# Moving the rebuild of x to VectorE and three small copies to GpSimd in a recurrent layer

## The chip, the cores and the metric

The kernel runs on one NeuronCore of one Trainium2 chip. The metric is device time in microseconds (us), from runs of the whole program on that core. A core has a matrix engine (TensorE, in the profile PE, with its weight loads as PEld) and four engines that matter beside it here: VectorE (DVE), ScalarE (ACT), GpSimd (POOL) and SyncE (SP), which only issues transfers in this kernel. Each engine works through its own list of instructions strictly in the order in which the list was built, and the lists wait for one another by semaphores. An instruction at the head of a list that has to wait holds up everything behind it on that engine.

## The reference, cut to what matters

One inference step of a two-layer decoder: 1024 prompt tokens and 8 sample tokens, so 1032 columns in all, at a width of 1024. Layer 0 is a recurrent block, layer 1 attention; each is followed by an MLP. The change sits in layer 0:

```python
u = x @ w_in
gate, xr = jnp.split(u, 2, axis=-1)
xc, conv_new = causal_conv(xr, conv_prev, conv_w, conv_b)     # width 4, and the last 3 rows as new state
r = sigmoid(xc @ w_a + b_a);  i = sigmoid(xc @ w_x + b_x)     # in 4 blocks of 256 channels
a = exp(-8 * r * softplus(-lam))
u = sqrt(1 - a*a) * (i * xc)
h = scan(h_t = a_t * h_{t-1} + u_t)                           # and the last h as new state
out = (h * gelu(gate)) @ w_out
```

Products are computed in full single precision by splitting each operand into a rounded high part and the rest (low part) and adding three products: high with high, high with low, low with high.

## The kernel before

Everything is kept transposed: 128 channels on the partitions, 1032 tokens along the row. The width is eight such tiles, called m = 0 to 7. A product of one output tile is 8 (or, in a gate block, 2) pieces along the depth times 3 passes times 3 chunks of 344 tokens, and its three chunks lie in three PSUM banks. There are two sets of three banks, "bP" and "bS, bS, bT", and the products take them in turn: while TensorE fills one set, the other has to be emptied, or TensorE waits.

The recurrent layer is a list of stages, written out by hand in `LRU` (lines 55 and 56), run in the order of that list:

- `x` m (`xr_stage`): the product of the input with w_in for tile m, 72 matmuls. VectorE empties the banks (line 1127) and GpSimd starts the convolution from the result (line 1128, three chunks).
- `c` m (`conv`): the other taps of the convolution on VectorE (line 1133 for the prompt, 1137 for the sample tokens), two small copies of state rows (lines 1134 and 1135), and the split of xc into high and low, the high part on ScalarE (line 253), the low on VectorE (line 254).
- `g` k (`gates`): four products of 18 matmuls each, for the two gates of the tiles 2k and 2k+1. ScalarE empties the banks with the sigmoid (line 1161).
- `r` k (`recur`): for two tiles: x = high + low (line 1170), i * x (1171), tanh, exp and squares on ScalarE (1173, 1175, 1180), a product on VectorE (1181), the square root (1183), the scan (1186 to 1189), and the copy of the last state (1190). The tanh writes over the tile that holds x, so it waits until line 1171 has read it.
- `o` m (`gate_out`): the gate product, 72 matmuls, emptied by VectorE (line 1199), then gelu and the product with the scan.

The stages in the order in which they are written are: c1 c0 x4 g0 c2 c3 r0 c4 x5 g1 c5 r1 x7 x6 g2 r2 c7 o5 c6 o0 o1 o3 g3 r3 o6 o2 o4 o7. A scheduler then builds the list of each engine from this program: it may put an instruction of a later stage ahead of one of an earlier stage, by its own estimate of when operands are ready, and by the priority that some stages ask for. So a change in one line can move others on all lists.

Weights arrive as tiles `raw` of 512 KB through two buffers in turn (`fetch`, line 159, issued on SP's queue). ScalarE rounds each into `wh` (line 165), an engine subtracts into `wl` (line 166: VectorE, for one unit in this stretch GpSimd), and then the buffer is free for the next transfer. The state rows leave through the same SP queue: `o_conv` twice (lines 1211 and 1212, they need the copies of all eight `c` stages; the last tile to come is m = 6) and `o_h` (line 1213). In the program these three stand behind r3; where they stand in SP's list is up to the scheduler.

Of the kernel before, what the change touches and what calls it, by code (L numbers as in the profile page):

```python
# [13 lines left out]
ALU = mybir.AluOpType  # L14
# [5 lines left out]
SEQ = 1024  # L20
NS = 8
T = SEQ + NS
# [37 lines left out]
def trunk(ctx: ExitStack, tc: tile.TileContext, I, O):  # L60
    nc = tc.nc
    pe, act, dve, pool, sp = nc.tensor, nc.scalar, nc.vector, nc.gpsimd, nc.sync
# [30 lines left out]
    def A(s="a"):  # L93
        return ap.tile([P, T], F32, tag="A", name=nm(s))
# [4 lines left out]
    def S(s="s"):  # L99
        return small["pool"].tile([P, CH], F32, tag="S", name=nm(s))  # L100
# [24 lines left out]
    def cs(c):  # L125
        return slice(c * CH, (c + 1) * CH)
# [12 lines left out]
    def V(n, m=0):  # L139
        o, _ = VEC[n]  # L140
        return vec[:, o + m:o + m + 1]
# [34 lines left out]
    for o in [("x", m) for m in range(4)] + LRU:  # L176
        if o[0] == "g":
            units.append(("gate", o[1], I["w_gate"][o[1]], W))
        elif o[0] in "xo":
            m = o[1] + (8 if o[0] == "x" else 0)  # L180
# [71 lines left out]
    def split_act_dve(hi, lo, src, sl, eng=dve):  # L252
        act.copy(r_(hi[:, sl]), src)
        eng.tensor_tensor(r_(lo[:, sl]), src, hi[:, sl], ALU.subtract)
# [834 lines left out]
    cst = cp.tile([P, M8, 4, NS], F32, name="cst")  # L1089
# [3 lines left out]
    cvp = cp.tile([P, M8, 3], F32, name="cvp")  # L1093
    hno = cp.tile([P, M8, 1 + NS], F32, name="hno")
# [23 lines left out]
    ys = {}  # L1118
# [11 lines left out]
    def conv(m):  # L1130
        xr, xc = xrc.pop(m)
        for d, w in ((1, "cw2"), (2, "cw1"), (3, "cw0")):
            dve.scalar_tensor_tensor(xc[:, d:SEQ], xr[:, 0:SEQ - d], V(w, m), xc[:, d:SEQ], ALU.mult, ALU.add)
        dve.tensor_copy(cst[:, m, 3, :], xr[:, SEQ:T])
        dve.tensor_copy(cvp[:, m, :], xr[:, SEQ - 3:SEQ])
        for k, w in ((2, "cw2"), (1, "cw1"), (0, "cw0")):
            dve.scalar_tensor_tensor(xc[:, SEQ:T], cst[:, m, k, :], V(w, m), xc[:, SEQ:T], ALU.mult, ALU.add)
        hi, lo = A("xch"), A("xcl")
        split_act_dve(hi, lo, xc, slice(0, T))
        xcs[m] = (hi, lo)  # L1140
# [23 lines left out]
    def recur(kb):  # L1164
        ms = (2 * kb, 2 * kb + 1)
        for m in ms:
            i = rr[m, 1]
            xh, xl = xcs.pop(m)
            ys[m] = (W if m in (2, 3, 5, 7) else A)("t")
            pool.tensor_tensor(ys[m], xh, xl, ALU.add)  # L1170
            pool.tensor_tensor(i, i, ys[m], ALU.mult)
        for m in ms:
            act.activation(ys[m], rr[m, 0], AF.Tanh, scale=sp8[:, m:m + 1])
        for m in ms:
            act.activation(rr[m, 0], rr[m, 0], AF.Exp, scale=nsp8[:, m:m + 1])
        for m in ms:
            r, t = rr[m, 0], ys[m]
            for c in range(NCH):
                a2 = S("a2")
                act.activation(a2, r[:, cs(c)], AF.Square)  # L1180
                dve.scalar_tensor_tensor(t[:, cs(c)], a2, 1.0, t[:, cs(c)], ALU.add, ALU.mult)
        for m in ms:
            act.activation(ys[m], ys[m], AF.Sqrt)
        for m in ms:
            r, i, t = rr.pop((m, 0)), rr.pop((m, 1)), ys[m]
            dve.tensor_tensor(i, t, i, ALU.mult)
            dve.tensor_tensor_scan(t[:, :SEQ], r[:, :SEQ], i[:, :SEQ], 0.0, ALU.mult, ALU.add)
            dve.tensor_tensor(t[:, SEQ:T], r[:, SEQ:T], h0[:, m, :], ALU.mult)
            dve.tensor_tensor(t[:, SEQ:T], t[:, SEQ:T], i[:, SEQ:T], ALU.add)
            dve.tensor_copy(hno[:, m, :], t[:, SEQ - 1:T])  # L1190

    gos = {}

    def gate_out(m):
# [9 lines left out]
        gos[m] = (hi, lo)  # L1204

    stages = {"x": xr_stage, "c": conv, "g": gates, "r": recur, "o": gate_out}
    xr_first()
    for what, i in LRU:
# [170 lines left out]
```

## Time and profile before

| | us |
|---|---|
| median of 3 runs | 2040.84 (2040.08 to 2043.04) |
| the profiled execution | 2038.14 |
| its span in the trace | 2036.3 |
| TensorE busy in the span | 2003.5 (98%) |
| VectorE, ScalarE, GpSimd busy | 1413.2, 1051.9, 352.5 |

The recurrent layer takes about the first 270 us of the span. In the rows of the profile, a line of the timeline gives the start in us from the span's start, how long the row's instructions took together, engine, line, operation, output and inputs, how many, and in brackets how long the engine had been idle before and what ended that. A row of the groups gives the busy time in all, the mean in ns of one, and the idle time before.

### The profile page before, as it was taken

How to read it: one execution, taken by the hardware profiler on the slowest of the kernel's cores; microseconds unless marked ns; L12 is line 12 of the kernel's file. 1: busy time of each engine (PE TensorE's matmuls, PEld its weight loads, DVE VectorE, ACT ScalarE, POOL GpSimd, SP SyncE). 2: the span in 40 equal slices, each digit the busy share in tenths (PEclk: the TensorE clock that was granted, in tenths of full speed). 3: DMA queues.
4: the chain of work that ended last, by engine and by line, in shares of the span. 5: the costliest groups of instructions: out<-in, count | busy, mean ns of one | idle time of the engine just before them, and what ended most of it. 6: DMA issues, size and time to landing. Idle time of an engine off the chain costs nothing.

```text
span 2036.3 us, 38639 instructions
## 1 busy us (share of the span) xinstructions
PE 2003.5 (98%) x15106; PEld 1957.5 (96%) x15106; DVE 1413.2 (69%) x2673; ACT 1051.9 (52%) x2090; POOL 352.5 (17%) x562
## 2 busy tenths in 40 slices
PE   9989999999999999999999999999999999999999
PEld 8989999999999999999988887999999999999999
DVE  8887537876766766766846777569766666777663
ACT  6475635544343655555457776555434435555450
POOL 2541100000001223221003434100000003323220
PEclk9989999999999999999999999999999999999999
DMA  5112142344445777877443435612543447887683
GB/s 175 52 32 55 53 167 84 105 154 143 148 139 197 233 216 213 230 178 179 129 108 84 106 99 175 234 63 83 171 157 130 162 167 235 218 224 219 166 200 105
DMA packets 121047, 304.87 MB, mean 150 GB/s; under 512 B 20888, under 2 KB 53152, under 8 KB 120864
## 3 DMA queue, kind: packets, MB, share of 16 engines
q1 hardware_dynamic: 64864, 135.41, 21.6%
q0 software_dynamic: 28352, 98.30, 19.0%
q10 hardware_dynamic: 27648, 68.70, 9.3%
q8 instruction: 118, 1.93, 0.4%
q14 instruction: 65, 0.53, 0.1%
HBM read 176.22 MB, written 113.44 MB: 142 GB/s over the span
## 4 chain that ended last, share of the span: by engine, by line
PE 84%; issue 4%; DMA 3%; DVE 2%; ACT 2%; POOL 1%; SPq 0%; POOLq 0%; ACTq 0%
PE bD L529 54%; PE bP L226 11%; PE bS L226 6%; PE bP L768 4%; PE bT L226 3%; PE bO L889 2%; PE bS L848 1%; PE bT L868 1%; PE bN L714 1%; DMA spill<-ho 1%; DMA spill<-he 1%; DMA tl<-hsum 1%; PE bS L796 1%; POOL t L1170 0%; POOL tl L542 0%
## 5 line engine op out<-in xcount | busy, mean ns | idle before, releaser
L529 PE MATMUL bD<-op,op 128*128 128x258 f32 x5376 | 648.5, 283 | 0.0
L529 PEld LDWEIGHTS bD<-op,op 128*128 128x128 f32 x5376 | 647.9, 189 | 0.3
L529 PE MATMUL bD<-tl,op 128*128 128x258 f32 x4704 | 570.1, 284 | 4.4 <-ACT ho L633 4.1
L529 PEld LDWEIGHTS bD<-tl,op 128*128 128x128 f32 x4704 | 568.5, 190 | 5.8 <-ACT ho L633 4.5
L542 POOL DMA_DIRECT2D tl<-hsum x196 | 115.5, 674 | 900.2 <-ACT ho L633 421.6
L396 DVE TENSOR_TENSOR op<-ws,op 128x512 fp32r<-128x512 f32 (+2 forms) x288 | 168.5, 598 | 84.2 <-ACT op L395 84.2
L633 ACT COPY ho<-bD 128x516 f32<-128x516 f32 x144 | 85.1, 591 | 226.8 <-PE bD L529 226.8
L402 DVE TENSOR_TENSOR tl<-tl 128x516 fp32r<-128x516 f32 x196 | 130.6, 692 | 93.5 <-ACT tl L401 89.8
L395 ACT CAST op<-ws 128x512 fp32r<-128x512 f32 (+2 forms) x288 | 153.4, 550 | 42.0 <-DVE op L396 23.4
L633 ACT COPY he<-bD 128x516 f32<-128x516 f32 x144 | 84.0, 583 | 167.6 <-PE bD L529 167.6
L396 DVE TENSOR_TENSOR op<-raw,op 128x512 fp32r<-128x512 f32 (+2 forms) x216 | 124.1, 597 | 62.6 <-ACT op L395 62.6
L395 ACT CAST op<-raw 128x512 fp32r<-128x512 f32 (+2 forms) x216 | 114.1, 549 | 43.6 <-PE bD L529 20.3
L401 ACT CAST tl<-tl 128x516 fp32r<-128x516 f32 x196 | 115.3, 627 | 3.5 <-DMA tl<-hsum 3.5
L646 ACT ACTIVATE ho<-ho 128x1032 f32<-128x1032 f32 x32 | 34.2, 1070 | 107.5 <-DVE ho L645 107.5
L166 DVE TENSOR_TENSOR wl<-raw,wh 128x1024 fp32r<-128x1024 f32 (+1 forms) x57 | 68.1, 1201 | 25.1 <-ACT wh L165 20.3
L641 DVE TENSOR_TENSOR ho<-bD,ho 128x516 f32<-128x516 f32 x72 | 49.9, 694 | 43.3 <-PE bD L529 43.3
L859 POOL TENSOR_SCALAR se<-se,den 128x256 f32<-128x256 f32 (+1 forms) x128 | 66.4, 524 | 76.3 <-DVE den L857 74.3
L165 ACT CAST wh<-raw 128x1024 fp32r<-128x1024 f32 (+1 forms) x60 | 58.6, 988 | 37.1 <-DMA raw<-w_in 15.3
L652 POOL DMA_DIRECT2D spill<-ho x32 | 28.7, 896 | 257.2 <-DVE ho L641 245.9
L852 DVE CUSTOM_DVE_ANT_0 se<-bS,bias,nsink 128x256 f32<-128x256 f32 (+1 forms) x128 | 56.4, 461 | 21.6 <-PE bS L848 16.8
L855 ACT ACTIVATE se<-se,den 128x257 f32<-128x257 f32 (+1 forms) x128 | 63.0, 496 | 14.8 <-DVE den L852 13.2
L637 DVE TENSOR_TENSOR ho<-bD,ho 128x516 f32<-128x516 f32 x72 | 49.8, 691 | 20.2 <-PE bD L529 13.1
(299 smaller groups left out, 3743.6 us busy)
## 6 DMA issues: line engine op xcount, KB each, us to landing
tl<-hsum POOLq DMA_DIRECT2D x196, 258.0 KB, 7.2
raw<-w_up SPq DMA_DIRECT2D x64, 512.0 KB, 3.7
raw<-w_dn SPq DMA_DIRECT2D x64, 384.0 KB, 6.6
spill<-ho POOLq DMA_DIRECT2D x32, 516.0 KB, 5.6
spill<-he POOLq DMA_DIRECT2D x32, 516.0 KB, 7.2
hsum<-ho ACTq DMA_DIRECT2D x28, 516.0 KB, 3.7
hsum<-he ACTq DMA_DIRECT2D x28, 516.0 KB, 2.7
hsum<-ts ACTq DMA_DIRECT2D x28, 516.0 KB, 3.4
```

What stands on the lines that cost most here:

```text
L166: eng.tensor_tensor(r_(lo[:, sl]), raw[:, sl], hi[:, sl], ALU.subtract)
L226: pe.matmul(o, lhsT=r_(wt[:, col(k):col(k) + P]), rhs=r_(xt[:, cs(c)]), start=(k == first and a == 0), stop=(k == final and a == 2))
L395: act.copy(r_(t[:, 0:n]), src)
L396: dve.tensor_tensor(r_(t[:, n:2 * n]), src, t[:, 0:n], ALU.subtract)
L401: act.copy(r_(hi), lo)
L402: dve.tensor_tensor(r_(lo), lo, hi, ALU.subtract)
L529: pe.matmul(d[:, 512 * b:512 * b + QT], lhsT=r_(wt[:, j * P:j * P + P]), rhs=r_(xt[:, QT * b:QT * b + QT]), start=first and j == 0 and a = ...
L542: pool.dma_start(t[:, n:2 * n], src)
L633: last["copy"] = act.copy(t, f).ins
L768: pe.matmul(ps[c], lhsT=r_(wt[:, k * P:k * P + P]), rhs=r_(xt[:, cs(c)]), start=(k == 0 and a == 0), stop=(k == M8 - 1 and a == 2))
L855: act.activation(se[:, u, 256 - n:257], se[:, u, 256 - n:257], AF.Exp, scale=-1.0, bias=dn[:, u:u + 1], accum_out=dn[:, 2 + u:3 + u])
L859: pool.tensor_scalar(e, e, dn[:, 2 + u:3 + u], 0.0, ALU.mult, ALU.add)
```

## The change

Two lines go from GpSimd to VectorE, three go the other way. The dependencies between the values stay as they are.

```diff
     def conv(m):
...
-        dve.tensor_copy(cst[:, m, 3, :], xr[:, SEQ:T])
-        dve.tensor_copy(cvp[:, m, :], xr[:, SEQ - 3:SEQ])
+        pool.tensor_copy(cst[:, m, 3, :], xr[:, SEQ:T])
+        pool.tensor_copy(cvp[:, m, :], xr[:, SEQ - 3:SEQ])
...
     def recur(kb):
...
-            pool.tensor_tensor(ys[m], xh, xl, ALU.add)
-            pool.tensor_tensor(i, i, ys[m], ALU.mult)
+            dve.tensor_tensor(ys[m], xh, xl, ALU.add)
+            dve.tensor_tensor(i, i, ys[m], ALU.mult)
...
-            dve.tensor_copy(hno[:, m, :], t[:, SEQ - 1:T])
+            pool.tensor_copy(hno[:, m, :], t[:, SEQ - 1:T])
```

Per tile m that is one addition and one product of 128 x 1032 for VectorE, and copies of 128 x 8, 128 x 3 and 128 x 9 for GpSimd; with eight tiles, 16 operations one way and 24 the other. The lists as built differ in other places too. On SP's list the two transfers `o_conv` now stand before the weights of o3 and g3 (they stood behind them). On ScalarE's list the sigmoids of g1 stand before most of the squares of r0, the rounding of g3's weights stands before the tanh of r2, and that of o1's between the first and second sigmoids of g2. On TensorE's list the last product of g1 is no longer mixed with the first matmuls of x7.

## The prediction

> **What bounds the kernel now.** I read the page's first part, then TensorE's timeline for gaps, then the lists of the engines that those gaps wait for.
>
> ```profile
> span 2036.3 us, 38639 instructions
> ...
> PE 2003.5 (98%) x15106; PEld 1957.5 (96%) x15106; DVE 1413.2 (69%) x2673; ACT 1051.9 (52%) x2090; POOL 352.5 (17%) x562
> ```
>
> TensorE is the bound: only 32.8 us of the span are not its busy time. A change off TensorE can win only from gaps, and from slow clock that follows gaps. In the recurrent layer these are its rows (timeline of TensorE, then the chain of waits for o5's 72 matmuls):
>
> ```profile
> 94.12 0.63 PE L226 MATMUL bP<-xch,wh 128*128 128x344 f32 x3
> ...
> 104.93 1.53 PE L226 MATMUL bP<-xch,wh 128*128 128x344 f32 x3 [4.99 <-ACT ri L1161]
> ...
> 143.43 1.08 PE L226 MATMUL bS<-xch,wh 128*128 128x344 f32 x2 [3.89 <-DVE xr L1127]
> ...
> 155.07 0.63 PE L226 MATMUL bP<-hh,wh 128*128 128x344 f32 x3
> ...
> 206.81 0.43 PE L226 MATMUL bP<-xch,wh 128*128 128x344 f32 x1 [0.59 <-ACT ri L1161]
> ```
> ```profile
> 155.24 11.33 PE bP L226 x72
> ```
>
> From the first matmul of g1 (94.12) to the first of o5 (155.07) pass 60.95 us, for g1, x7, x6 and g2: 288 matmuls, at 11.33 per 72 equal to 45.3. So 15.6 us are lost here; behind it, up to the MLP, only 0.59. Of the 15.6, 8.9 are two gaps, one inside g1 and one inside g2. Most of the rest is slow clock (stretches of 5 us; the column after POOL is the granted clock):
>
> ```profile
> 100.00:105.00 5.00, 0.07 (x1) 0.07 (x1) 3.85 (x7) 4.97 (x10) 4.25 (x4) 0.71 0.00 0
> 105.00:110.00 5.00, 4.98 (x18) 4.39 (x18) 5.00 (x10) 4.94 (x7) 0.00 (x0) 0.61 0.01 3
> ...
> 140.00:145.00 5.00, 1.57 (x4) 1.30 (x5) 5.00 (x8) 0.68 (x2) 1.52 (x2) 0.81 0.23 48
> 145.00:150.00 5.00, 5.00 (x19) 5.00 (x19) 4.98 (x9) 2.35 (x4) 5.00 (x4) 0.51 0.41 162
> ```
>
> After each gap the clock is at half for 6.8 us (5 x 0.29 + 5 x 0.39 = 3.4 us of missing clock; 5 x 0.19 + 5 x 0.49 likewise). What falls into TensorE's work is about 2.0 after the first gap (5 x 0.39, it restarts at 104.93) and 3.2 after the second (2.45, and half of the 1.57 before it): 2.6 on average.
>
> **The gap in g1.** It waits for ScalarE's sigmoid, and ScalarE for GpSimd (timelines of ScalarE and GpSimd):
>
> ```profile
> 83.98 2.96 ACT L253 CAST xch<-xc 128x1032 fp32r<-128x1032 f32 x3
> 93.68 1.16 ACT L1173 ACTIVATE t<-ri,sp 128x1032 f32<-128x1032 f32 x1 [6.74 <-POOL ri L1171]
> 96.07 1.16 ACT L1173 ACTIVATE t<-ri,sp 128x1032 f32<-128x1032 f32 x1 [1.23 <-POOL ri L1171]
> 97.25 1.28 ACT L1175 ACT_TABLE_LOAD   x1
> 98.54 2.20 ACT L1175 ACTIVATE ri<-ri,nsp 128x1032 f32<-128x1032 f32 x2
> 100.65 2.37 ACT L1180 ACTIVATE a<-ri 128x344 f32<-128x344 f32 x6
> 103.03 1.28 ACT L1161 ACT_TABLE_LOAD   x1
> 104.33 1.42 ACT L1161 ACTIVATE ri<-bP,vec 128x344 f32<-128x344 f32 x3
> ...
> 107.06 1.06 ACT L1183 ACTIVATE t<-t 128x1032 f32<-128x1032 f32 x1
> ```
> ```profile
> L1171 POOL TENSOR_TENSOR ri<-ri,t 128x1032 f32<-128x1032 f32 x8 | 23.5, 2948 | 12.9 <-ACT ri L1161 12.8
> L1170 POOL TENSOR_TENSOR t<-xch,xcl 128x1032 f32<-128x1032 f32 x8 | 21.2, 2649 | 58.3 <-PE bT L226 41.1 <-issue 10.3 <-ACT ri L1161 4.4
> ```
> ```profile
> L1187 DVE TENSOR_TENSOR_SCAN t<-ri,ri 128x1024 f32<-128x1024 f32 x8 | 18.2, 2282 | 0.0
> ...
> L1186 DVE TENSOR_TENSOR ri<-t,ri 128x1032 f32<-128x1032 f32 x8 | 9.6, 1230 | 4.8 <-ACT t L1183 4.8
> ```
>
> VectorE's price for a moved operation is that of L1186, the same operation on the same shape: 1.23, at most GpSimd's 2.65 to 2.95; I take 1.2, the former, as it is the same engine. In the list as built, VectorE subtracts the low parts of tiles 2 and 3 first (each needs its ScalarE cast, the first of which ends at 85.0), then the four moved operations of r0: 85.0 + 2 x 1.2 + 4 x 1.2 = 92.2, the first product at 91.0. The two tanhs then end at 93.4 instead of 97.23, 3.8 earlier. ScalarE's list also has five of the six squares behind the sigmoids now (5/6 of 2.37 = 2.0). So the first sigmoid of g1 starts at 104.33 - 3.8 - 2.0 = 98.5 and empties its bank by 99.0; TensorE needs it at 99.9. Gap and slow clock go, with 0.9 us to spare.
>
> **The gap in g2.** VectorE empties x6's banks late, being blocked meanwhile (timelines of GpSimd and VectorE):
>
> ```profile
> 136.47 2.98 POOL L166 TENSOR_TENSOR wl<-raw,wh 128x1024 fp32r<-128x1024 f32 x1 [8.85 <-PE bS L226]
> ```
> ```profile
> 137.16 2.31 DVE L1188 TENSOR_TENSOR t<-ri,h 128x8 f32<-128x8 f32 x1
> ...
> 141.74 1.21 DVE L166 TENSOR_TENSOR wl<-raw,wh 128x1024 fp32r<-128x1024 f32 x1
> 142.87 0.92 DVE L1127 TENSOR_TENSOR xr<-bS,rt 128x344 f32<-128x344 f32 x2
> ```
>
> An operation on eight columns takes 2.31 us and ends with GpSimd's (136.47 + 2.98): the two exclude one another. [...]
>
> After the change, from 98.5 on ScalarE works without a pause up to the square roots of r1: four sigmoid triples (4 x 1.42), 11 squares (4.35), five table loads (6.4), four square roots (4.24), two casts (2.1), two tanhs (2.3), two exps (2.2), together 27.3: 125.8. Their inputs are there in time: TensorE's next products end at 102.6, 105.4; VectorE's product of r1 for tile 3 needs only the sigmoid at 109.9, so 1.2 later. Then one product and the scan (1.2 + 2.28) bring VectorE to 129.4, and in the list as built x6's banks come next, freed at 129.9 to 130.8. TensorE needs them at 94.12 + 11.33 x 3 + 2.83 = 130.9. No gap, with nothing to spare; half a microsecond more is possible.
>
> **What is late next.** On SP's list `o_conv` twice now precedes o3's weights, and on ScalarE's list the rounding of these weights precedes the third sigmoid of g2, whose banks o5 needs. Before, o3's weights went alone (lists of SP and ScalarE, groups of transfers, and the last busy stretch behind `o_conv`):
>
> ```profile
> raw<-w_in SPq DMA_DIRECT2D x9, 512.0 KB, 3.7
> ...
> o_conv<-cst SPq DMA_DIRECT2D x1, 96.0 KB, 7.1
> ```
> ```profile
> 146.60 1.05 ACT L165 CAST wh<-raw 128x1024 fp32r<-128x1024 f32 x1 [5.91 <-DMA raw<-w_in]
> ```
> ```profile
> 160.36 0.64 SPq L1211 DMA_DIRECT2D o_conv<-cst  x1
> ...
> 162.22 26.79 SPq L159 DMA_DIRECT2D raw<-w_in  x4
> ```
> ```profile
> 169.00:170.00 1.00, 1.00 (x8) 1.00 (x7) 1.00 (x3) 0.99 (x2) 0.00 (x0) 1.00 0.05 21
> ```
>
> The weights' buffer comes free when VectorE has subtracted o0's low part: 130.8, the second scan 2.28, small ones 0.3, 1.21: 134.6. Alone, the transfer was ready for ScalarE 3.65 after that point (141.74 + 1.21 to 146.60): 138.3. Behind `o_conv` the transfer issued at 162.22 moved data until about 169.4, so 7.2: 141.8. I take the latter: `o_conv` can go as soon as GpSimd has copied x6's rows, about 1 us after 130.8, so it is some 2 us ahead of the weights, as at 160.36 and 162.22. Then 1.05 for the rounding and half a microsecond for a sigmoid: o5 starts at 143.4. TensorE is free at 94.12 + 45.3 = 139.4: a new gap of 4.0, as long as the old ones, with the same clock price, 2.6. [...] The two old gaps agree (4.99 and 3.89, both paid); whether a shorter one pays, this trace doesn't show.
>
> **The copies.** 24 copies on GpSimd, each between VectorE's price and that of GpSimd's smallest row (groups of VectorE, timeline of GpSimd):
>
> ```profile
> L1134 DVE COPY cst<-xr 128x8 f32<-128x8 f32 x6 | 1.0, 160 | 0.0
> ```
> ```profile
> 125.77 1.86 POOL L1128 TENSOR_SCALAR xc<-xr,vec 128x344 f32<-128x344 f32 x3 [3.46 <-DVE xr L1127]
> ```
>
> 0.16 to 0.62 each, and up to one scan (2.28) of waiting for VectorE. GpSimd was busy 17%, which hides them. Queued behind them are line 1128 of the next tile (VectorE's list needs the same scans first, so no cost) and the subtraction for o1, needed 23 us after o5 starts. Only x6's two copies count, ahead of `o_conv`: if they wait for the second scan, `o_conv` leaves at about 134 to 136 and the weights up to 2.7 later. VectorE saves under 0.2 per copy: nothing on the path. In g3 the moved addition of r3 goes ahead of line 1199: 0 to 1.2 on the gap of 0.59; I take 0.3, since GpSimd no longer runs there beside VectorE.
>
> **The sum.** o5 starts at 143.4 instead of 155.07: 11.7 saved, less 2.6 of clock and 0.3 in g3: 8.8. Against the profiled execution (2036.3 span, 1.8 around it, 2038.1) that is 2029.3. This execution lies 2.7 below the median of 2040.84; on the scale of the median it is 2032.0.
>
> **The rivals.** (a) The weights come early enough. Alone (3.65) they leave a gap of 0.5 and no slow clock: 155.07 - 139.9 - 0.3 = 14.9 saved, 2026. [...] For it: `o_conv` may pass sooner. Against it: the transfer at 162.22.
> (b) VectorE is later than I reckon, by ordinary waits. Each microsecond up to 134.6 moves the weights by as much and thus the end, whatever g2's gap does: 4 us later leaves 4.8, time 2036; 8.8 leaves nothing, 2041. VectorE was at 5.00 of 5 us in two of the stretches shown.
> (c) Slower: the moved operations cost on VectorE what they cost on GpSimd. Eight of them lie before 134.6: 8 x (2.8 - 1.2) = 12.8 later, less 8.8: 4 us slower, 2045. It decides from 1.2 + 8.8/8 = 2.3 us each. L1186 (1.23) speaks against it; that some 8-column operations took 2.31 there speaks for it.
>
> **How the numbers follow.** My forecast 45%, (a) 25%, (b) 18%, (c) 12%. The time is the first case's, 2032.0; its own range is 2028 to 2035 (2.7 later weights, a gap just short of the limit). The range of 2025 to 2039 takes in (a) and (b) up to some 7 us, and leaves out (c) and the rest of (b), under 2 in 10. Changes within 0.2% (4.1 us, about what runs spread over 3 us can tell) are the end of (b): faster 0.77, same 0.12, slower 0.11.
>
> **What would show it.** Right: no TensorE gap in g1, first tanh near 91; x6's banks emptied at about 130; one gap before o5 that waits for L1161, with ScalarE's L165 just before it waiting for the transfer; one half-clock stretch instead of two; L1170 and L1171 near 1.2 on VectorE. Wrong: L1170 above 2 us there, a g1 gap that remains (ScalarE 1 us later than reckoned), or the weights within 4 us.

## The result and the profile after

The changed kernel takes 2036.76 us (median of 22 runs, 2032.75 to 2040.17) against 2040.70 for the kernel before, run beside it 22 times (2036.54 to 2043.23). The ratio is 0.9982, 95% interval 0.9975 to 0.9988: 2.4 to 5.1 us faster, 3.7 in the middle. The forecast was 8.8 faster. The direction was right; less than half of the gain came. The profiled execution took 2034.74 us.

First the line of the engines on the page of the changed kernel, then TensorE's timeline at its two gaps in this layer, and its stretches of 5 us around the larger one (the column after POOL is the granted clock):

```profile
PE 2000.6 (98%) x15106; PEld 1955.8 (96%) x15106; DVE 1411.6 (69%) x2665; ACT 1050.7 (52%) x2089; POOL 323.1 (16%) x570
```
```profile
147.72 1.53 PE L226 MATMUL bP<-hh,wh 128*128 128x344 f32 x3 [8.09 <-ACT ri L1161]
201.78 0.42 PE L226 MATMUL bP<-xch,wh 128*128 128x344 f32 x1 [0.66 <-ACT ri L1161]
```
```profile
140.00:145.00 5.00, 0.00 (x0) 0.00 (x0) 4.43 (x6) 0.00 (x0) 1.42 (x1) 0.68 0.89 89
145.00:150.00 5.00, 2.28 (x7) 1.98 (x8) 2.48 (x3) 3.83 (x8) 0.00 (x0) 0.50 0.41 135
150.00:155.00 5.00, 5.00 (x28) 5.00 (x27) 3.42 (x3) 4.98 (x5) 0.00 (x0) 0.80 0.25 96
```

Both old gaps (4.99 in g1, 3.89 in g2) are gone, and one new gap stands ahead of o5, 8.09 long. The layer's last gap, in g3, is reached at 201.78 instead of 206.81: 5.03 earlier.

The way up to the new gap, in the timelines of VectorE and ScalarE:

```profile
87.36 2.37 DVE L1170 TENSOR_TENSOR t<-xch,xcl 128x1032 f32<-128x1032 f32 x2
89.65 2.37 DVE L1171 TENSOR_TENSOR ri<-ri,t 128x1032 f32<-128x1032 f32 x2
...
129.77 0.91 DVE L1127 TENSOR_TENSOR xr<-bS,rt 128x344 f32<-128x344 f32 x2
130.60 0.50 DVE L1127 TENSOR_TENSOR xr<-bT,rt 128x344 f32<-128x344 f32 x1
...
131.10 2.28 DVE L1187 TENSOR_TENSOR_SCAN t<-ri,ri 128x1024 f32<-128x1024 f32 x1
...
133.76 1.21 DVE L166 TENSOR_TENSOR wl<-raw,wh 128x1024 fp32r<-128x1024 f32 x1
...
134.97 1.27 DVE L1133 SCALAR_TENSOR_TENSOR xc<-xr,vec,xc 128x1021 f32<-128x1021 f32 x1
```
```profile
90.97 2.24 ACT L1173 ACTIVATE t<-ri,sp 128x1032 f32<-128x1032 f32 x2 [2.38 <-DVE ri L1171]
...
98.42 1.43 ACT L1161 ACTIVATE ri<-bP,vec 128x344 f32<-128x344 f32 x3
...
146.18 1.04 ACT L165 CAST wh<-raw 128x1024 fp32r<-128x1024 f32 x1 [11.07 <-DMA raw<-w_in]
```

A moved operation costs 1.2 on VectorE. The buffer for o3's weights is free at 133.76 + 1.21 = 135.0. But ScalarE gets these weights only at 146.18, after 11.07 of waiting. What lies between is in the timelines of GpSimd and SP (the two rows of line 1128 at 130.46 and 133.81 overlap: the second shows the last of the three operations alone):

```profile
117.27 1.86 POOL L1128 TENSOR_SCALAR xc<-xr,vec 128x344 f32<-128x344 f32 x3 [0.21 <-DVE xr L1127]
...
130.46 6.12 POOL L1128 TENSOR_SCALAR xc<-xr,vec 128x344 f32<-128x344 f32 x3 [11.06 <-DVE xr L1127]
136.53 0.19 POOL L1134 COPY cst<-xr 128x8 f32<-128x8 f32 x1
136.66 0.19 POOL L1135 COPY cvp<-xr 128x3 f32<-128x3 f32 x1
```
```profile
133.81 2.78 POOL L1128 TENSOR_SCALAR xc<-xr,vec 128x344 f32<-128x344 f32 x1
```
```profile
136.75 0.64 SPq L1211 DMA_DIRECT2D o_conv<-cst  x1
...
138.20 0.61 SPq L159 DMA_DIRECT2D raw<-w_in  x1
```

Three operations of line 1128 take 1.86 us for x7 and 6.12 for x6, where VectorE works without a pause from one operation with two inputs to the next (busy 5.00 of the 5 us from 130, and 4.98 of the next 5). The two copies that `o_conv` needs stand behind them on GpSimd and end at 136.72 and 136.85; the two `o_conv` leave at 136.75 and 137.43, and the weights of o3 behind it on SP's list at 138.20, 3.2 after their buffer was free. Then they share the transfer engines with `o_conv`, and from 141.45, when SP issues them, with the next 512 KB of weights (`w_gate`) too; they need 7.98 until ScalarE starts.

### The profile page after: what moved, and what is told of

It reads as the page before. It is cut to its first block, busy times and chain, and to the rows that moved or that the text cites. A ratio compares the mean times of both kernels' runs of the same rounds, so it can differ in the third digit from the quotient of the medians.

```text
span 2032.6 us, 38634 instructions
## 1 busy us (share of the span) xinstructions
PE 2000.6 (98%) x15106; PEld 1955.8 (96%) x15106; DVE 1411.6 (69%) x2665; ACT 1050.7 (52%) x2089; POOL 323.1 (16%) x570
## 3 DMA queue, kind: packets, MB, share of 16 engines
q1 hardware_dynamic: 64864, 135.41, 21.5%
## 4 chain that ended last, share of the span: by engine, by line
PE 89%; issue 4%; DMA 3%; DVE 2%; ACT 1%; POOL 1%; SPq 0%; ACTq 0%; POOLq 0%; DVEq 0%
PE bD L529 54%; PE bP L226 13%; PE bS L226 7%; PE bP L768 4%; PE bT L226 3%; PE bO L889 2%; PE bS L848 1%; PE bT L868 1%; PE bN L714 1%; DMA spill<-ho 1%; DMA spill<-he 1%; DMA tl<-hsum 1%; DVE sq L277 1%; PE bS L796 1%; DMA raw<-w_in 0%
## 5 line engine op out<-in xcount | busy, mean ns | idle before, releaser
L641 DVE TENSOR_TENSOR ho<-bD,ho 128x516 f32<-128x516 f32 x72 | 49.9, 693 | 42.9 <-PE bD L529 42.9
L226 PE MATMUL bP<-hh,wh 128*128 128x344 f32 x216 | 54.5, 328 | 9.7 <-ACT ri L1161 8.1
```

Of the source, the lines that this page charges most:

```text
L226: pe.matmul(o, lhsT=r_(wt[:, col(k):col(k) + P]), rhs=r_(xt[:, cs(c)]), start=(k == first and a == 0), stop=(k == final and a == 2))
```

## The experiments

The theory after the result: VectorE is on time; the copies on GpSimd, behind a GpSimd that can hardly get in beside VectorE (6.12 us for line 1128 instead of 1.86), hold `o_conv`, and `o_conv` holds the weights by the order of SP's list. The rivals: VectorE, with sixteen more operations, is late by itself; or `o_conv`'s place costs nothing, and the loss is in the transfer or elsewhere.

**All copies back on VectorE, the rebuild of x stays there.** On SP's list `o_conv` then stands behind the weights again.

```diff
-        pool.tensor_copy(cst[:, m, 3, :], xr[:, SEQ:T])
-        pool.tensor_copy(cvp[:, m, :], xr[:, SEQ - 3:SEQ])
+        dve.tensor_copy(cst[:, m, 3, :], xr[:, SEQ:T])
+        dve.tensor_copy(cvp[:, m, :], xr[:, SEQ - 3:SEQ])
...
-            pool.tensor_copy(hno[:, m, :], t[:, SEQ - 1:T])
+            dve.tensor_copy(hno[:, m, :], t[:, SEQ - 1:T])
```

> The rebuild of x is on VectorE as in the changed kernel, all three kinds of copies stay on VectorE, and the two transfers o_conv stand behind the weights of o3 and g3 on SP's list, as before. Theory: what ate the gain of the changed kernel is the copies on GpSimd alone, by way of o_conv, which they hold back, and the weights of o3 that stand behind o_conv. Then those weights are issued at about 135, land in some 3.7 us, TensorE's gap ahead of o5 is under 1.5 us instead of 8.09, no stretch around 140 to 155 has a clock under 0.9, and the time is 8 to 11 us below the changed kernel, 12 to 15 us below the kernel before (ratio about 0.9935). Rival: VectorE, fuller by sixteen operations, is late for o3's weights by itself; then the gap stays above 4 us, the clock still drops, and the time stays within 3 us of the changed kernel.

Measured: 2026.29 us, ratio to the kernel before 0.9936 (0.9924 to 0.9948). Timelines of SP, ScalarE and TensorE of this run:

```profile
135.50 0.33 SPq L159 DMA_DIRECT2D raw<-w_in  x1
```
```profile
139.16 1.05 ACT L165 CAST wh<-raw 128x1024 fp32r<-128x1024 f32 x1 [3.54 <-DMA raw<-w_in]
```
```profile
140.70 1.30 PE L226 MATMUL bP<-hh,wh 128*128 128x344 f32 x3 [0.55 <-ACT ri L1161]
193.18 0.43 PE L226 MATMUL bP<-xch,wh 128*128 128x344 f32 x1 [0.65 <-ACT ri L1161]
```

The weights are issued at 135.50 and used 3.66 later, the gap is 0.55, the clock from 135 to 160 stays at 1.00. VectorE, with all its old copies and the sixteen new operations, is not late. The copies, together with the place on SP's list that `o_conv` took when they moved, cost some 9 us; between this run and the changed kernel the lists of TensorE and ScalarE are the same in this layer, and VectorE's and GpSimd's differ in the copies and in the place of line 1137 behind them.

**Only the two copies of tile 6 on ScalarE**, `o_conv` still ahead of o3's weights:

```diff
-        pool.tensor_copy(cst[:, m, 3, :], xr[:, SEQ:T])
-        pool.tensor_copy(cvp[:, m, :], xr[:, SEQ - 3:SEQ])
+        f = act.copy if m == 6 else pool.tensor_copy
+        f(cst[:, m, 3, :], xr[:, SEQ:T])
+        f(cvp[:, m, :], xr[:, SEQ - 3:SEQ])
```

(in this run the lines from here on have a number one higher)

> The changed kernel, but the two copies of tile 6 alone, for which o_conv waits, are done by ScalarE; o_conv still stands ahead of o3's weights on SP's list. Theory: GpSimd can hardly read the on-chip memory while VectorE works without a pause, which stretched three operations of line 1128 for x6 to 6.12 us and held the copies behind them. Without it o_conv leaves at 132 to 133, the weights are issued at about 135, when VectorE has freed their buffer, instead of 138.2; but they move beside o_conv and take 7 to 8 us. The gap ahead of o5 is 4 to 5.5 us instead of 8.09, still with a slow clock: 2.5 to 4 us faster than the changed kernel, ratio to the kernel before about 0.9967. Rival: o_conv is late for another reason (SP's own list); then the weights are issued at 138 still, the gap stays at 8, and the time is that of the changed kernel. Second rival: o_conv costs the weights nothing once it is early; then they land 3.7 us after their issue, the gap is under 1.5, and the time is 8 us or more below the changed kernel.

Measured: 2030.91 us, ratio 0.9959 (0.9946 to 0.9971). Timelines of SP, ScalarE and TensorE of this run:

```profile
131.50 0.64 SPq L1212 DMA_DIRECT2D o_conv<-cst  x1
...
135.08 0.33 SPq L159 DMA_DIRECT2D raw<-w_in  x1
```
```profile
141.92 1.04 ACT L165 CAST wh<-raw 128x1024 fp32r<-128x1024 f32 x1 [5.40 <-DMA raw<-w_in]
```
```profile
143.46 1.30 PE L226 MATMUL bP<-hh,wh 128*128 128x344 f32 x3 [3.51 <-ACT ri L1162]
```

GpSimd's three operations of line 1128 are as slow as in the changed kernel (6.11), but nobody waits for them. `o_conv` leaves 5.2 earlier and the weights at 135.08, when VectorE has freed their buffer. They still take 6.84 beside `o_conv`, and the gap is 3.51. This separates the two parts of the loss: 8.09 to 3.51 is the late GpSimd, 3.51 to 0.55 is `o_conv`'s place among the transfers. The prediction's own case, "a new gap of 4.0", is what this run shows.

**`o_conv` issued by GpSimd behind its own copies**, all other orders but SP's as in the changed kernel:

```diff
-            sp.dma_start(O["conv"][:, :, 3:27].rearrange("p m (k n) -> p m k n", k=3), cst[:, :, 1:4, :])
-            sp.dma_start(O["conv"][:, :, 0:3], cvp)
+            pool.dma_start(O["conv"][:, :, 3:27].rearrange("p m (k n) -> p m k n", k=3), cst[:, :, 1:4, :])
+            pool.dma_start(O["conv"][:, :, 0:3], cvp)
```

> The changed kernel with the two transfers o_conv issued by GpSimd right behind its copies instead of by SP; TensorE's, VectorE's and ScalarE's lists are the same. The weights of o3 no longer stand behind o_conv. Theory: the wait on SP's list was most of the loss; the weights are issued at about 135, ahead of o_conv (about 137). If they keep that start and land before o_conv takes its share, in 3.7 to 5 us, the gap ahead of o5 is 0.5 to 2 us, the clock stays up, and the time is 7 to 11 us below the changed kernel. If o_conv's small packets push in beside them they take 7 us, the gap is about 4 us, with a slow clock, and the gain over the changed kernel is 3 to 5 us. Rival: the order on SP's list does not matter, since the weights wait for VectorE anyway; the gap stays at 8 and the time is that of the changed kernel.

Measured: 2025.86 us, ratio 0.9931 (0.9913 to 0.9950), the fastest median of the study, though its interval overlaps that of the first experiment. Timelines of GpSimd, SP, ScalarE and TensorE:

```profile
136.63 1.07 POOL L1211 DMA_DIRECT2D o_conv<-cst  x1 [0.19 <-POOL cvp L1135]
```
```profile
134.60 0.33 SPq L159 DMA_DIRECT2D raw<-w_in  x1
```
```profile
138.25 1.05 ACT L165 CAST wh<-raw 128x1024 fp32r<-128x1024 f32 x1 [3.54 <-DMA raw<-w_in]
```
```profile
139.79 1.30 PE L226 MATMUL bP<-hh,wh 128*128 128x344 f32 x3 [0.57 <-ACT ri L1161]
```

The copies are as late as in the changed kernel, and so is `o_conv` (136.63). The weights, 2 us ahead of it now, take 3.65, as if it were not there. In stretches of 1 us their 512 KB have moved by 138.0 (57, 262 and 205 GB/s from 135 on), and the bytes of `o_conv` only then (82 and 28): the two never met. So these weights, ahead of `o_conv`, did not pay for it; what the two cost each other where they move together and the weights were issued first, this run does not show.

**`o_conv` at the end of the layer on SP's list**, copies on GpSimd:

```diff
-            sp.dma_start(O["conv"][:, :, 3:27].rearrange("p m (k n) -> p m k n", k=3), cst[:, :, 1:4, :])
-            sp.dma_start(O["conv"][:, :, 0:3], cvp)
             sp.dma_start(O["h"], hno)
+    tc.keep_in_program_order(sp.dma_start(O["conv"][:, :, 3:27].rearrange("p m (k n) -> p m k n", k=3), cst[:, :, 1:4, :]))
+    tc.keep_in_program_order(sp.dma_start(O["conv"][:, :, 0:3], cvp))
```

> The changed kernel with the two transfers o_conv put at the end of the layer on SP's list, behind the weights of the next product; the copies stay on GpSimd, and VectorE's, ScalarE's and GpSimd's orders are those of the changed kernel. Theory: the copies harm only by way of o_conv's place. GpSimd's line 1128 for x6 still takes about 6 us and the copies still come at 136 to 137, but nobody waits for them: o3's weights are issued at 134.5 to 135.2 and land in some 3.7 us, the gap ahead of o5 is 0.5 to 0.8, and the time is 12 to 15 us below the kernel before (ratio about 0.9934). Rival: late copies cost something by themselves (the subtraction for o1 behind them on GpSimd, VectorE blocked beside it); then a new wait appears behind o5 and the time is 3 us or more above that of the run with all copies on VectorE.

Measured: 2028.50 us, ratio 0.9949 (0.9934 to 0.9964). TensorE's timeline:

```profile
139.84 1.30 PE L226 MATMUL bP<-hh,wh 128*128 128x344 f32 x3 [0.46 <-ACT ri L1161]
192.33 0.42 PE L226 MATMUL bP<-xch,wh 128*128 128x344 f32 x1 [0.66 <-ACT ri L1161]
```

In the layer it is as fast as the run before it (192.33 and 192.28 at the last gap): late copies cost nothing by themselves. The whole is some 2 us behind the first experiment and misses the expected 12 to 15 (it gains 10); the intervals overlap, and why is not settled.

**The copies alone**, the rebuild left on GpSimd:

```diff
-        dve.tensor_copy(cst[:, m, 3, :], xr[:, SEQ:T])
-        dve.tensor_copy(cvp[:, m, :], xr[:, SEQ - 3:SEQ])
+        pool.tensor_copy(cst[:, m, 3, :], xr[:, SEQ:T])
+        pool.tensor_copy(cvp[:, m, :], xr[:, SEQ - 3:SEQ])
...
-            dve.tensor_copy(hno[:, m, :], t[:, SEQ - 1:T])
+            pool.tensor_copy(hno[:, m, :], t[:, SEQ - 1:T])
```

(lines against the kernel before; its lists on SP, TensorE and ScalarE do not change)

> The kernel before with the three kinds of copies on GpSimd and nothing else; the rebuild of x stays on GpSimd. SP's, TensorE's and ScalarE's lists are those of the kernel before, so o_conv stays behind the weights. Theory: the copies cost next to nothing by themselves, and harm only through o_conv's place: the time is within 0.1% of the kernel before, both gaps (4.99 and 3.89) stay within 1 us. Rival: the copies take GpSimd's time where ScalarE waits for it (the first tanh at 93.7) and delay g1's first sigmoid by 1 to 3 us: 1 to 3 us slower.

Measured: 2037.67 us, ratio 0.9997 (0.9988 to 1.0006). The gaps are 4.66 and 3.87. So the same 24 copies cost nothing where `o_conv` stays behind the weights, though x6's come late here too: its operations of line 1128 start at 144.21, its copies at 150.56.

**The rebuild for r0 alone, and for r1 alone**, copies as before (in these two runs the lines from 1170 on have a number one higher, so L1171 is the addition):

```diff
-            pool.tensor_tensor(ys[m], xh, xl, ALU.add)
-            pool.tensor_tensor(i, i, ys[m], ALU.mult)
+            e = dve if kb == 0 else pool
+            e.tensor_tensor(ys[m], xh, xl, ALU.add)
+            e.tensor_tensor(i, i, ys[m], ALU.mult)
```

(the other run has `kb == 1`)

> The kernel before with the rebuild of x and its product moved to VectorE for r0 alone; all copies stay on VectorE, o_conv stays behind the weights of o3 and g3. Theory: the first gap (4.99, in g1) belongs to r0's two lines on GpSimd, and goes, with its slow clock: 6 to 8 us at that place. What the second gap (3.89, in g2) does then tells whether it is a wait of its own: if r1's lines on GpSimd set when VectorE frees x6's banks, it stays between 3 and 7, and the time is 4 to 8 us below the kernel before (ratio 0.996 to 0.998). Rival: the second gap only follows from the late r0; then both are gone and the time is that of the run in which the whole rebuild is on VectorE, about 13 below.

> The kernel before with the two lines moved for r1 alone, copies and o_conv as before. Theory: the first gap stays at about 5 with its slow clock, since r0 still runs on GpSimd; the second, in g2, falls under 1.5 us, because VectorE is no longer blocked and no longer waits for r1's product: 4 to 7 us below the kernel before (ratio 0.9965 to 0.998). Rival: the second gap stays above 3, because x6's banks are late for r0's sake; then the time is within 2 us of the kernel before.

Measured: r0 alone 2035.23 us, ratio 0.9978 (0.9969 to 0.9988); r1 alone 2039.60 us, ratio 1.0001 (0.9991 to 1.0010). Timelines of VectorE, GpSimd and TensorE with r0 moved, then of TensorE and VectorE with r1 moved:

```profile
87.34 6.88 DVE L1171 TENSOR_TENSOR t<-xch,xcl 128x1032 f32<-128x1032 f32 x2
...
135.41 0.91 DVE L1127 TENSOR_TENSOR xr<-bS,rt 128x344 f32<-128x344 f32 x2
```
```profile
86.43 6.70 POOL L1171 TENSOR_TENSOR t<-xch,xcl 128x1032 f32<-128x1032 f32 x2 [9.79 <-DVE xcl L254]
```
```profile
98.14 0.85 PE L226 MATMUL bS<-xch,wh 128*128 128x344 f32 x2 [1.05 <-DVE xr L1127]
103.52 1.30 PE L226 MATMUL bP<-xch,wh 128*128 128x344 f32 x3 [1.75 <-ACT ri L1161]
```
```profile
98.15 0.84 PE L226 MATMUL bS<-xch,wh 128*128 128x344 f32 x2 [1.41 <-DVE xr L1127]
105.47 1.52 PE L226 MATMUL bP<-xch,wh 128*128 128x344 f32 x3 [2.16 <-ACT ri L1161]
...
142.87 0.84 PE L226 MATMUL bS<-xch,wh 128*128 128x344 f32 x2 [3.14 <-DVE xr L1127]
```
```profile
142.32 0.92 DVE L1127 TENSOR_TENSOR xr<-bS,rt 128x344 f32<-128x344 f32 x2
```

Neither expectation held whole. With r0 moved both large gaps go, the second too (0.51 is left at 135.96), which was the rival's case, yet the time falls by 4.5 us and not by 13. With r1 moved the second gap stays at 3.14, the rival's case, and nothing is won on the whole. The two halves add up to 4 us, and both together are worth 13. The rows give two reasons, and not the whole account.

The first is the price. VectorE's two additions take 6.88 instead of 2.37 while GpSimd does its own two (6.70) beside them, so a moved operation cost 1.2 where GpSimd did none of these at the same time, and 3.4 where it did. With r0 moved six shorter gaps are left (1.05, 1.75, 0.51, 0.48, 0.79 and 0.82), and the layer's last gap is reached at 199.98: 6.83 earlier than before, where the first experiment has 13.63. The rest, from 6.83 in the layer to 4.5 on the whole, lies behind it; this profile has slow clock there too (0.83 from 860 to 870, 0.55 from 1330 to 1340; see the repeats).

The second reason is an order. With r0 moved, as in the changed kernel, VectorE's list empties x6's banks right behind the first scan of r1 (135.41). In the kernel before and with r1 moved alone, the second scan and a subtraction (line 166) stand ahead of that (142.32). With r1 moved the first scan ended at 136.70 and x6's product at 136.92; had the banks come next, they would have been empty by about 138.3 (136.92 and the 1.4 that the emptying takes), ahead of 139.73, where TensorE stopped. That is an estimate from these rows. By it the second gap hangs on the place that the scheduler gave line 1127 rather than on r0 or r1 as such; no run changes that place alone.

**The disputed cost by itself**: three operations of GpSimd behind the end of the kernel before, alone and beside a row of VectorE's. `side` first lets VectorE copy GpSimd's input, so that both start together; `big` is line 1128's operation, `little` a copy of 128x8; beside them run nothing, six products, six operations with one input, or three scans:

```diff
+    for f in (big, little):
+        for beside in (None, two, one, scan):
+            side(f, beside)
```

> The kernel before with a measurement behind its end: three operations of GpSimd (multiply and add with a column, 128x344, as line 1128; then three copies of 128x8) are run alone, beside six products of VectorE (both inputs in SBUF, 128x1032), beside six operations of VectorE with one input (128x1032), and beside three scans (128x1032). Theory: VectorE's operations with two inputs in SBUF, one behind the other, shut GpSimd out. Alone the three take about 1.9 us (copies about 0.5 in all); beside the products and the scans they take 5 to 8 us, about as long as VectorE's row of operations, the small copies too; beside operations with one input 1.9 to 2.5. Rival: the two engines share the memory's speed; then everything beside VectorE, with one input as with two, is slower by the same factor, about 1.5 to 2, and a copy of eight columns loses under 0.3 us. The time of the whole is that of the kernel before plus the measurement, 50 to 90 us, and tells nothing.

Timelines of GpSimd and VectorE behind the end, in the order of the two loops:

```profile
2040.14 1.83 POOL L1262 TENSOR_SCALAR po<-pq,vec 128x344 f32<-128x344 f32 x3 [52.15 <-DVE pq L1255]
2042.80 4.70 POOL L1262 TENSOR_SCALAR po<-pq,vec 128x344 f32<-128x344 f32 x3 [0.83 <-DVE pq L1255]
2051.82 3.09 POOL L1262 TENSOR_SCALAR po<-pq,vec 128x344 f32<-128x344 f32 x3 [4.32 <-DVE pq L1255]
2057.63 7.73 POOL L1262 TENSOR_SCALAR po<-pq,vec 128x344 f32<-128x344 f32 x3 [2.72 <-DVE pq L1255]
2066.16 0.44 POOL L1265 COPY po<-pq 128x8 f32<-128x8 f32 x3 [0.80 <-DVE pq L1255]
2067.40 2.40 POOL L1265 COPY po<-pq 128x8 f32<-128x8 f32 x3 [0.79 <-DVE pq L1255]
...
2080.36 4.48 POOL L1265 COPY po<-pq 128x8 f32<-128x8 f32 x3 [3.56 <-DVE pq L1255]
```
```profile
2042.62 8.49 DVE L1269 TENSOR_TENSOR wa<-wa,wb 128x1032 f32<-128x1032 f32 x6
```

The kernel with this took 2091.65 us. The three take 1.83 alone, 4.70 beside products and 7.73 beside scans; three copies of eight columns 0.44, 2.40 and 4.48. A common factor is out: beside products the three large operations take 2.6 times as long, the three copies 5.5 times, and beside scans each copy loses 1.3 us, not under 0.3. But the theory, in the form "shut out for the whole row", is out too: beside products GpSimd was done after 4.70 of VectorE's 8.49. The rows fit turns: GpSimd's operation waits until VectorE's present one ends, takes its turn, and the next waits again (beside products its first ends at 2044.34, 0.5 behind the product that ends at 2043.84, and its third at 2047.50, 0.5 behind the one that ends at 2047.00). Six products would take 7.2 alone; 8.49 is some 1.3 more, so VectorE waits too. Operations with one input hold GpSimd up also (3.09, and 1.32 for the copies), which the theory had not expected. For x6 this gives about what the trace has: three operations of 0.6, the second held by a scan (2.28), the third by the subtraction and an operation of the convolution (1.21 + 1.27; it took 2.78). That the third did not get in between these two shows that the turn is not always taken at the first end; the runs do not tell why.

**Repeats**, to tell what belongs to one execution (the kernels as they are):

> The kernel before once more, for its clock behind the recurrent layer. In the first profile it has one piece of half clock there, at about 1890. Theory: these late pieces, each worth about 1.7 us, belong to the execution and not to the kernel; then they are elsewhere or absent here, while the two gaps of the layer (4.99 and 3.89) are within 0.3 us of the first profile. Rival: they are fixed by the kernel's timing; then the one piece is at 1890 again.

> The changed kernel once more. In the first profile pieces of half clock at about 865 and 1330 took back 1.4 and 1.6 us of the 5.0 saved in the layer. Theory: they belong to the execution; here they are elsewhere, or fewer or more, and the gap ahead of o5 is 8.1 again within 0.4. Rival: what the change moves in time brings them; then they are at 865 and 1330 again, and with them the difference between the layer's saving and the whole's is explained.

> The run with all copies on VectorE once more. In its first profile the layer saved 13.6 us, and pieces of half clock at about 1320 to 1340 took back some 4. Theory: they belong to the execution; here they differ by at least one piece of 1.7 us. Rival: they are at the same place with the same size.

Measured: the gaps return (4.95 and 3.88 before, 7.90 after, 0.28 with all copies on VectorE). For the clock, stretches of 10 us at one of the late places, the first of the changed kernel's first profile, the other two of its repeat:

```profile
1330.00:1340.00 10.00, 10.00 (x63) 9.94 (x63) 3.93 (x9) 3.48 (x7) 0.00 (x0) 0.83 0.09 33
```
```profile
1330.00:1340.00 10.00, 10.00 (x54) 9.72 (x53) 3.92 (x7) 3.52 (x7) 0.00 (x0) 0.69 0.10 35
1340.00:1350.00 10.00, 9.22 (x48) 8.94 (x47) 5.54 (x30) 3.38 (x12) 0.00 (x0) 0.79 0.05 19
```

A stretch of 10 us at 0.83 has lost 10 x 0.17 = 1.7. Theory and rival are each half right. Most places return (about 860 and 1330 after, 1890 before, both times; the repeat of the kernel before has one more at 1340, that of the run with all copies on VectorE one more at 850), but the size does not: 1.7 at 1330 in one execution of the changed kernel, 5.2 in the other, and with all copies on VectorE about 5 once and 1.7 once. The times of single executions thus differ by one to three such pieces. Why the clock drops at 1330, where TensorE is busy 10.00 of 10, stays open.

## Why the prediction was wrong

Its steps, in order:

| step | predicted | measured |
|---|---|---|
| first product of r0 on VectorE done, first tanh | 91.0 | 90.97 |
| first sigmoid of g1; gap in g1 | 98.5; none | 98.42; none |
| x6's banks emptied; gap in g2 | 129.9 to 130.8; none | 129.77 to 131.10; none |
| buffer for o3's weights free | 134.6 | 134.97 |
| x6's rows copied, `o_conv` can go | about 1 us after 130.8 | 136.85 |
| o3's weights issued | 134.6 | 138.20 |
| their rounding starts | 141.8 | 146.18 |
| o5 starts; gap | 143.4; 4.0 | 147.72; 8.09 |
| clock lost in TensorE's work | 2.6 | 2.1 |
| more wait in g3 | 0.3 | 0.07 |

**What was right.** The walk along ScalarE and VectorE through two stages holds to 0.4 us. Both old gaps went, and what was named as late next was late next: `o_conv` ahead of o3's weights, then the rounding, then the sigmoid. Of the second gap the prediction named the smaller cause: the block of 2.31 was 2.2 of the 5.6 us between the end of the first scan and the emptying of x6's banks, and the rest was the order of VectorE's list. It reckoned with the new order, taken from the list as built, but did not name it as what ends the gap. In the changed kernel the blocked operation (line 1188, at 131.02) takes 0.15; the subtraction of GpSimd's that stood beside it (line 166) comes there only at 139.08. Rival (c), VectorE as dear as GpSimd, was rightly set aside for the whole change (1.23 and 1.23 on average, lines 1170 and 1171); the run with r0 alone shows what would have made it true. Rival (b), VectorE late by ordinary waits, did not come: 0.4 us.

**What failed** is one term, in the step "What is late next": "`o_conv` can go as soon as GpSimd has copied x6's rows, about 1 us after 130.8". It came 6 us after. Under "The copies" the prediction did say that they might wait, but for one scan, "and the weights up to 2.7 later"; it took that into the range and left it out of the sum. It counted the wait of the copies and not those of the three operations of line 1128 ahead of them on GpSimd, of which the second waited for a scan of VectorE's and the third for two shorter operations. "No cost" was said of line 1128 behind the copies; the cost was in line 1128 ahead of them. The trace of the kernel before already had the price (timeline of GpSimd):

```profile
143.48 0.63 POOL L1128 TENSOR_SCALAR xc<-xr,vec 128x344 f32<-128x344 f32 x1 [4.03 <-DVE xr L1127]
144.07 2.38 POOL L1170 TENSOR_TENSOR t<-xch,xcl 128x1032 f32<-128x1032 f32 x1
146.44 3.37 POOL L1128 TENSOR_SCALAR xc<-xr,vec 128x344 f32<-128x344 f32 x2
```

x6's three operations span 6.3 us there as well (143.48 to 149.81), 2.4 of them an addition of GpSimd's own and 3.37 for two operations that take 0.6 each alone; the row that the prediction showed, 1.86, is x7's.

So the weights were issued 3.2 after their buffer was free instead of at once; the buffer was 0.4 late, and the transfer took 7.98 instead of 7.2: together 4.4 later at the rounding, 4.3 at o5. Whether these 0.8 come from `o_conv`, closer ahead than reckoned, or from `w_gate`'s 512 KB, under way from 141.45, the runs do not separate. That this term was the one that failed shows in the run with x6's copies on ScalarE, where `o_conv` goes early: it gains 8.4 us (5.9 to 11.0) against the 8.8 of the sum. The sum with the measured terms: 155.07 - 147.72 = 7.35, less 2.1 (the restart at 147.72 falls into 2.28 us at half clock and 5 us at 0.80) and 0.07, is 5.2; the layer's last gap shows 5.03. The whole gains 3.7, within 2.4 to 5.1: in the profiled pair one piece of half clock more (two late ones against one, 1.7) is about the rest.

**Rival (a)**, "alone (3.65) they leave a gap of 0.5", was the right price for a case that the kernel missed by an order on a list. It was given 25% and 2026 us; where the weights do not stand behind `o_conv`, the runs give gaps of 0.55, 0.57 and 0.46, and 2026.29, 2025.86 and 2028.50 us. The prediction's own range counts in "a gap just short of the limit": no run shows such a limit. Gaps of 3.51 and 3.14 cost 1.7 us of clock each, those of 0.46 to 0.57 none.

## What to carry to other kernels

Where work moves from GpSimd to VectorE, look at what is left on GpSimd at that time: here one operation of line 1128 lost a whole scan (2.28), and three took 6.12 us instead of 1.86, so count them one by one along the list, small copies and whatever stands ahead of them included. Then ask who waits for the last of them; here it was not an engine but a small transfer at the head of a queue, with the next weights behind it. Moving such a transfer behind the weights, or to the queue of the engine that makes its data, turned a gain of 0.2% into one of 0.5 to 0.7%. And where a scheduler builds the lists, compare them before a gap's end is put down to the operation that was moved: here the emptying of x6's banks also changed its place.

## What the runs showed of the hardware that was not expected

**Slow clock comes in pieces, and not by the length of one gap alone.** The loss, as the sum of the missing clock over stretches of 5 us, is 5 x (0.32 + 0.50 + 0.20) = 5.1 us behind the gap of 8.09, 3.4 behind the 4.99 and the 3.89 of the kernel before, and 1.7 behind 3.87, 3.51 and 3.14 of other runs, and behind the 3.88 of the repeat of the kernel before: once, twice or three times 1.7, which is 3.4 us at half clock (0.50 is granted in each stretch of 1 us from 103 to 108 of the kernel before). With r1 moved alone, even two gaps of 1.41 and 2.16, some 5 us apart, were followed by a loss of 5 x (0.04 + 0.30 + 0.34) = 3.4, while 1.05 and 1.75 at the same place, with r0 moved alone, cost no clock. So these runs show no firm limit: the longest gap of this layer that cost no clock is 1.75, the shortest single one that paid is 3.14, and 3.88 and 3.89 cost 1.7 and 3.4.

**A short operation is no protection.** Three copies of 128x8 on GpSimd cost 0.44 us alone and 4.48 beside scans.

**A load behind small packets.** The 512 KB of o3's weights took 3.54 to 3.67 from issue to rounding with `o_conv` behind them or far away, 6.84 with `o_conv` issued 3.6 ahead and 7.98 with it 1.5 ahead (7.78 in the repeat). In the two longest cases the next 512 KB were issued 3.3 behind the weights and moved beside their end. `o_conv` is 108 KB in small pieces: in the kernel before, 2080 of the 2098 packets from 158 to 165 are under 512 B.
